# The opening of layer one: the forgetting values are projected first, 512 columns wide and one k at a time, from tokens in 256-column chunks

## The chip, the core and the metric

The kernel runs on one core of a Trainium2 chip. A time is the device time of one launch in microseconds. The core has five instruction streams that run side by side and wait for each other by semaphores: PE (TensorE: matrix products and transposes), DVE (VectorE), ACT (ScalarE), POOL (GpSimd) and SP (SyncE, which only starts transfers). In tables PEld is PE's loading of the stationary operand. Each engine takes its instructions strictly in the order in which they were written, so an instruction that waits holds up all behind it.

## The reference, cut to what matters

A decoder trunk of two layers works on 256 tokens of 1024 channels. Each layer normalises the stream, multiplies it by one wide input matrix, cuts the product into the inputs of three token mixers and their gates, and closes with branch and output projections:

```python
for layer in range(DEPTH):                       # 2
    h = rms_norm(x, norm_w[layer])               # x * rsqrt(mean(x^2) + eps) * norm_w
    proj = einsum('bsd,de->bse', h, w_in[layer]) # 1024 x 12832 columns
    (a_xbc, a_z, a_dt, b_q, b_k, b_v, b_z, c_q, c_k, c_v, c_f, c_z, gates) = split(proj)
    y_a = mamba2_branch(...)
    y_b = sliding_window_branch(b_q, b_k, b_v, b_z, ...)
    y_c = forgetting_attention_branch(c_q, c_k, c_v, c_f, c_z, ...)
    branch = einsum('bsiw,iwd->bsid', stack([y_a, y_b, y_c]), w_proj[layer])
    merged = sum(sigmoid(gates + gate_bias) * branch)
    x = x + einsum('bsd,de->bse', merged, w_out[layer])
return rms_norm(x, final_norm_w)
```

Two column groups matter here: `b_v`, the 256 sliding-window values, and `c_v`, the 1024 forgetting values (the first 512 of them above all).

## The kernel before

**Products in three parts.** Everything is float32. An operand is cut in a high part that PE's fast format holds exactly and a low part, the rest; a product of two such operands is high·high + low·high + high·low, three matrix products for each block of 128 channels. There are eight such blocks, numbered k = 0 to 7. Weights arrive in `raw` tiles of 512 KB (four k of 256 columns or two k of 512); ACT writes the high part `hi`, DVE subtracts it and writes `lo`. A `raw` buffer is free for the next transfer when its `lo` is written; there are six.

**Tokens.** The two token blocks (t = 0, 1) of 128 tokens come in as rows, in the tile `x0`. PE transposes them against the identity `ident`, DVE multiplies the transposed block by the norm weights (into `xw`), ACT writes the high part `y0.hTh`, DVE the low part `y0.hTl`. In order listings these three tiles have the pool's name L and a number, as have all tiles of a shared pool. Only later, when the sums of squares are done, is the row factor `y0.rn` known; the first projections are scaled by it when they leave PSUM, and `normalize` then multiplies `xw` by it for all that follow.

**The order of work.** The opening of the program is written out by hand for all engines in a `manual_schedule` block: small functions issue one step each. `turn` transposes, `high` and `low` write the parts of the tokens, `w_high` and `w_low` those of half a weight tile, `square` sums squares, `hh`, `lh`, `hl` issue matrix products. `parts` are the first weight tiles; `first` are the two PSUM tiles (one per token block) that the first projection fills. Those products are only evicted later, through the list `late`. After that block the projections run from the list `ops`, one after another: `u_bv` makes sliding-window values, `u_cv` forgetting values, `u_gate` gates, `u_bk` the first rotated keys. `release` returns buffers of weight parts; `load_to` and `load_part` start weight transfers on SP. The rest of the program (some 95% of the time) is ordered by the same list and by a planner that puts attention steps between projections.

**The opening before.** SP first loads token block 0 in two transfers of 512 columns, then weights, then token block 1 whole. PE spends the time until the tokens land on seven transposes of the identity (`WARM`), and ten more (`FILL`) between the tokens' transposes and the first product. The first projection is `b_v`, 256 columns: token block 0 runs through k = 0 to 3 and 4 to 7, with the transposes of block 1 in its middle, then token block 1. Then come `c_v` columns 0 to 255 and 256 to 511, 256 at a time, the gates of the sliding-window branch 512 columns at a time, two transposes of the rotation table, and the keys.

Of the kernel before, what the change touches and what calls it, by code (L numbers as in the profile page):

```python
# [11 lines left out]
F32 = mybir.dt.float32  # L12
# [22 lines left out]
WARM = 7  # L35
FILL = 10
# [14 lines left out]
def hybrid_trunk(  # L51
# [131 lines left out]
    nc.scalar.dma_start(nw8, norm_w[0:1, :].rearrange("o (k p) -> (o k) p", p=P))  # L183
    tab = T("tab", [P, 1])
    nc.vector.memset(tab, 0.0)
    act(tab, tab, AF.Exp)
    x0 = T("L8", [P, 2, D])
    for j in range(2):
        nc.sync.dma_start(x0[:, 0, j * 512:(j + 1) * 512], x2[0:P, j * 512:(j + 1) * 512])
# [10 lines left out]
    one = T("L1", [P, P])  # L200
    nc.gpsimd.memset(one, 1.0)
    onesr = T("ones", [P, P], F32R)
    nc.gpsimd.tensor_copy(onesr, one)
    ones = onesr.bitcast(F32)

# [70 lines left out]
    def ordered(ap):  # L276

        return ap.rearrange("p (i a) -> p a i", a=2)
# [245 lines left out]
    def u_bv(y, t, placed=None):  # L524

        def f(w):
            p = tok(y.hTh, y.hTl, w, t, mid=pump) if placed is None else ordered(placed[t][:, 0:w.n])
            if t == 0:
                y.bv = T("bias", [P, 2, 256])
            (late.append if placed is not None else lambda g: g())(lambda: evict(p))  # L530

        def evict(p):
# [494 lines left out]
    def u_cv(y, c, t, i=None):  # L1027

        def f(w):
            p = tok(y.hTh, y.hTl, w, t)  # L1030
            if y.cv is None:
                y.cv = T("L8", [P, 2, D])
            m = w.n if i is None else w.n - 16
# [237 lines left out]
    for y in layers:  # L1271
# [11 lines left out]
        def cols(c0, n=256):  # L1283
            return sub([(0, w[:, c0:c0 + n])], n)
# [140 lines left out]
    with tc.manual_schedule(engines={ENG.PE, ENG.DVE, ENG.Activation, ENG.Pool}):  # L1425
        load_to(2)
# [3 lines left out]
        load_to(N_RAW)  # L1430
        warm = pmx()
        for i in range(WARM):
            transpose(warm[:, 0:P], ident, ident)


        nwT = T("L1", [P, NK])
        p = pmx()
        transpose(p[:, 0:NK], nw8, ident[:NK, :NK])
        nc.vector.tensor_copy(nwT, p[:, 0:NK])
# [3 lines left out]
        ss = T("ss", [P, 4], bufs=4)  # L1443

        def turn(t, j):
            p = pmx()
            for k in range(4):
                c = j * 512 + k * P
                transpose(p[:, k * P:(k + 1) * P], x0[:, t, c:c + P], ident)
            ks = slice(4 * j, 4 * j + 4)  # L1450
            tt(xw[:, t, ks, :], p.rearrange("p (k t) -> p k t", k=4), bc(nwT[:, ks], 2, P), op=ALU.mult)

        def high(t, j):
            ks = slice(4 * j, 4 * j + 4)
            act(y0.hTh[:, t, ks, :], xw[:, t, ks, :], AF.Copy)

        def low(t, j):
            ks = slice(4 * j, 4 * j + 4)
            tt(y0.hTl[:, t, ks, :], xw[:, t, ks, :], y0.hTh[:, t, ks, :].bitcast(F32), op=ALU.subtract)
# [15 lines left out]
        parts = [new_part() for _ in range(4)]  # L1475
        first.extend((pmx(), pmm()))

        def keys(t, k0, a, b, ends=False):

            for k in range(k0, k0 + 4):  # L1480
                mm(first[t][:, 0:256], a[:, t, k, :], in_turn(b(k)),
                   start=(k == 0 and a is y0.hTh and not ends), stop=(k == NK - 1 and ends))

        w0 = pieces[0]

        def hh(t, k0):
            keys(t, k0, y0.hTh, w0.hi)

        def lh(t, k0):
            keys(t, k0, y0.hTl, w0.hi)  # L1490

        def hl(t, k0):
            keys(t, k0, y0.hTh, w0.lo, True)

        square(0, 0)
        turn(0, 0)
        high(0, 0)
        w_high(parts[0], 0)
        turn(0, 1)
        for i in range(FILL):  # L1500
            transpose(warm[:, 0:P], ident, ident)
        low(0, 0)
        w_high(parts[0], 1)
        high(0, 1)
        w_low(parts[0], 0)
        w_low(parts[0], 1)
        w_high(parts[1], 0)
        w_high(parts[1], 1)
        low(0, 1)
        w_low(parts[1], 0)  # L1510
        w_low(parts[1], 1)
        hh(0, 0)
        lh(0, 0)
        hl(0, 0)
        hh(0, 4)
        turn(1, 0)
        turn(1, 1)
        lh(0, 4)
        square(0, 1)
        high(1, 0)  # L1520
        high(1, 1)
        low(1, 0)
        low(1, 1)
        hl(0, 4)
        hh(1, 0)
        lh(1, 0)
        hl(1, 0)
        hh(1, 4)
        lh(1, 4)
        hl(1, 4)  # L1530
        for i in range(2):
            w_high(parts[2], i)
            w_low(parts[2], i)
        square(1, 0)
        square(1, 1)
# [5 lines left out]
        for part in parts[3:]:  # L1541
            for i in range(2):
                w_high(part, i)
                w_low(part, i)
# [8 lines left out]
        release(pieces[0], 2)  # L1553
# [38 lines left out]
```

## Time and profile before

| | |
|---|---|
| median of three runs | 806.76 us (806.67 to 806.95) |
| span of the profiled execution, first to last instruction | 805.1 us |
| what lies around the span (median less span) | 1.7 us |
| PE busy | 796.5 us, 99% of the span, 5160 products |
| DVE busy | 684.2 us, 85% |
| ACT busy | 533.8 us, 66% |
| POOL busy | 167.5 us, 21% |
| moved from memory | 154.71 MB, 195 GB/s over the span |

The profile gives no time of its own for the profiled execution but its span, so the 1.7 us around it are taken as the same in every run. In a timeline row the first number is the start in us from the span's start, the second the time until the group's last instruction ended, then engine, source line, operation, tiles (written<-read), shapes, and the count. Idle time ahead of a row stands in brackets with what ended it. Durations of matrix products overlap: the time one costs is the distance between two starts.

### The profile page before, as it was taken

To read this page: it belongs to the slowest core of one execution; us is meant where nothing else is said; L and a number is where in the kernel's file an instruction comes from. 1 tells how busy PE (TensorE), PEld (TensorE's weight loads), DVE (VectorE), ACT (ScalarE), POOL (GpSimd) and SP (SyncE) were. 2 spreads that over 40 slices of the span, in tenths; PEclk is the share of its full clock that TensorE was granted. 3 is DMA by queue.
4 is the path that set the end of the run, shared out by engine and by line. 5 is a ranking of instruction groups with operands and counts; after the bars stand their busy time and mean duration, and the time that the engine had idled before them with its cause. 6 is when DMAs were issued, how large, how long until landed. Compare 5 with 4: busy or idle time off the path is not lost.

```text
span 805.1 us, 14840 instructions
## 1 busy us (share of the span) xinstructions
PE 796.5 (99%) x5160; PEld 711.6 (88%) x5160; DVE 684.2 (85%) x1416; ACT 533.8 (66%) x1146; POOL 167.5 (21%) x236
## 2 busy tenths in 40 slices
PE   9999999999999999999999999999999999999996
PEld 8998988888998988888998899888889989888896
DVE  6878999997998997795785799999889999969865
ACT  7776768875775885543665678687657768755452
POOL 3166213140210100033001741122311220002000
PEclk9999999999999999999999999999999999999999
DMA  9997987797765565686678987679976546576632
GB/s 316 280 259 172 253 219 200 219 290 220 198 184 167 174 187 170 219 253 205 217 251 257 239 210 217 157 217 287 285 211 196 183 143 202 156 248 210 209 106 78
DMA packets 138827, 170.43 MB, mean 212 GB/s; under 512 B 9353, under 2 KB 106465, under 8 KB 138753
## 3 DMA queue, kind: packets, MB, share of 16 engines
q1 hardware_dynamic: 114960, 140.53, 55.5%
q0 software_dynamic: 13328, 13.29, 10.3%
q10 hardware_dynamic: 10464, 15.67, 6.7%
q8 instruction: 41, 0.67, 0.3%
q14 instruction: 34, 0.27, 0.1%
HBM read 154.71 MB, written 2.16 MB: 195 GB/s over the span
## 4 chain that ended last, share of the span: by engine, by line
PE 91%; issue 3%; DMA 2%; POOL 2%; DVE 1%; ACT 1%; POOLq 0%; DVEq 0%
PE mm L109 78%; PE mx L109 9%; PE mx L113 4%; DMA L<-L 1%; DMA hb<-in_sinks_dram 1%; POOL L L488 1%; DMA L<-in_x_dram 0%; DVE L L551 0%; ACT pp L610 0%; POOL L L285 0%; POOL L L562 0%; DVE lo L291 0%; POOL sm L224 0%; POOL L L571 0%; POOL L L572 0%
## 5 line engine op out<-in xcount | busy, mean ns | idle before, releaser
L109 PE MATMUL mm<-L,hi 128*128 128x512 f32 x1056 | 354.7, 387 | 0.5 <-ACT L L487 0.3
L291 DVE TENSOR_TENSOR lo<-raw,hi 128x1024 fp32r<-128x1024 f32 (+1 forms) x276 | 313.3, 1154 | 40.9 <-ACT hi L290 36.1
L109 PE MATMUL mm<-hi,L 128*128 128x512 f32 (+2 forms) x1168 | 303.1, 349 | 0.1
L290 ACT ACTIVATE hi<-raw 128x1024 fp32r<-128x1024 f32 (+1 forms) x276 | 265.6, 982 | 50.6 <-PE mm L109 30.0
L109 PE MATMUL mm<-L,lo 128*128 128x256 f32 x1056 | 266.6, 273 | 0.0
L109 PEld LDWEIGHTS mm<-hi,L 128*128 128x128 f32 x1168 | 205.8, 190 | 23.2 <-issue 1.5
L109 PEld LDWEIGHTS mm<-L,hi 128*128 128x128 f32 x1056 | 195.1, 190 | 27.4 <-issue 3.0
L109 PEld LDWEIGHTS mm<-L,lo 128*128 128x128 f32 x1056 | 202.1, 191 | 5.3
L109 PE MATMUL mm<-lo,L 128*128 128x512 f32 (+2 forms) x584 | 201.5, 347 | 0.0
L109 PEld LDWEIGHTS mm<-lo,L 128*128 128x128 f32 x584 | 110.2, 190 | 10.7
L488 POOL DMA_DIRECT2D L<-L x68 | 60.7, 915 | 192.5 <-ACT L L487 155.2
L1074 POOL TENSOR_SCALAR_AFFINE_SELECT bias<-bias 128x128 f32<-128x128 f32 x64 | 30.8, 513 | 82.7 <-DMA bias<-cumd 82.7
L829 DVE SCALAR_TENSOR_TENSOR L<-L,vec,L 128x255 f32<-128x255 f32 (+2 forms) x96 | 46.2, 481 | 1.9 <-ACT L L826 0.4
L486 ACT ACTIVATE L<-mm 128x256 f32<-128x256 f32 x84 | 31.9, 380 | 20.0 <-PE mm L109 14.0
L652 ACT ACTIVATE pp<-pp,nm 128x128 f32<-128x128 f32 x64 | 28.2, 443 | 22.8 <-DVE nm L646 22.8
L1109 ACT ACTIVATE L<-L 128x512 f32<-128x512 f32 x24 | 15.1, 631 | 34.5 <-DVE L L1106 30.8
L610 ACT ACTIVATE pp<-pp,nm 128x128 f32<-128x128 f32 x32 | 12.6, 394 | 24.9 <-DVE nm L615 24.1
L488 POOL DMA_DIRECT2D qt<-L x16 | 14.2, 925 | 71.4 <-ACT qt L487 64.6
L1142 POOL TENSOR_TENSOR L<-L,L 128x512 f32<-128x512 f32 x8 | 12.0, 1494 | 74.0 <-DVE L L1141 74.0
L487 ACT ACTIVATE L<-mm 128x256 f32<-128x256 f32 x68 | 26.2, 386 | 1.5 <-DMA L<-L 1.5
L1106 DVE TENSOR_TENSOR L<-mm,L 128x512 f32<-128x512 f32 x22 | 15.1, 687 | 11.2 <-PE mm L109 11.2
L551 DVE TENSOR_TENSOR L<-L,cs 128x256 f32<-128x256 f32 x40 | 20.0, 536 | 4.6 <-DMA L<-L 4.6
(213 smaller groups left out, 913.7 us busy)
## 6 DMA issues: line engine op xcount, KB each, us to landing
raw<-in_w_in_dram SPq DMA_DIRECT2D x191, 512.0 KB, 5.1
raw<-in_w_proj_dram SPq DMA_DIRECT2D x48, 512.0 KB, 6.0
L<-L POOLq DMA_DIRECT2D x72, 128.0 KB, 5.4
raw<-in_w_out_dram SPq DMA_DIRECT2D x16, 512.0 KB, 5.9
bias<-cumd ACTq DMA_DIRECT2D x16, 256.0 KB, 3.4
L<-cumd ACTq DMA_DIRECT2D x8, 512.0 KB, 5.4
L<-in_gate_bias_dram ACTq DMA_DIRECT2D x12, 256.0 KB, 5.4
qt<-L POOLq DMA_DIRECT2D x16, 128.0 KB, 6.0
```

The lines of the kernel that those rows point to most:

```text
L109: nc.tensor.matmul(o, a, b, **kw)
L113: nc.tensor.transpose(o, a, i)
L290: keep(act)(hi, src, AF.Copy)
L291: keep(tt)(lo, src, hi.bitcast(F32), op=ALU.subtract)
L486: act(halves(lo), ordered(p[:, S:2 * S]), AF.Copy)
L487: last = act(halves(out), ordered(p[:, 0:S]), AF.Copy)
L488: nc.gpsimd.dma_start(out, lo, accum_op=ALU.add)
L551: tt(m, p, cs[:, i, :], op=ALU.mult)
L652: act(pp[:, i, sl], pp[:, i, sl], AF.Exp, scale=-1.0, bias=nm[:, e:e + 1], accum_out=sums[:, e:e + 1])
L829: stt(a[:, s:S], x_[:, 0:S - s], y.vec[:, 16 * j + u:16 * j + u + 1], a[:, s:S], op0=ALU.mult, op1=ALU.add)
L1074: nc.gpsimd.affine_select(out=bias[:, i, dst], in_=bias[:, i, src], compare_op=ALU.is_ge, fill=NEG, base=0, pattern=[[-1, P]], channel_mul ...
L1106: tt(halves(g), p, halves(y.gb), op=ALU.add)
```

## The change

Six things are edited, all in the opening of layer one; the order of all later work is as before, apart from where two small products of `normalize` fall.

- **What is projected first.** The first two PSUM tiles now hold `c_v`, 512 columns at once, instead of `b_v`, 256 columns. `b_v` follows it, 256 columns wide, as an ordinary projection; `c_v`'s eviction is the late one (`u_cv` takes `placed`, `u_bv` loses it). The first weights are so 2 MB instead of 1 MB, in four parts of two k each (`FIRST`), each part loaded as two transfers of one k, the very first on ACT's queue.
- **By single k.** Products run one k at a time, for both token blocks (`both`), instead of four k for one block.
- **Tokens.** They are loaded as 256, 256 and 512 columns of both blocks, between the weight transfers, and transposed, weighted and split in chunks of 256 columns (two k): `turn`, `weigh`, `high`, `low` of chunk c.
- **Warming.** The identity transposes are gone. Instead `stir` multiplies a constant tile of ones by itself, 256 columns wide, eight, three and two times, between the first transposes.
- **Constants.** The tile of ones is made by DVE at the start instead of by POOL after other masks, and ACT's loading of its function table stands behind its first two transfers.
- **Evictions.** The first evictions are two of 512 columns; `b_v`'s are behind them.

```diff
-WARM = 7
-FILL = 10
+WARM = (8, 3, 2)
+FIRST = 4
...
+one = T("L1", [P, P])
+nc.vector.memset(one, 1.0)
+onesr = T("ones", [P, P], F32R)
+nc.vector.tensor_copy(onesr, one)
...
-        step_ = kper // 2 if j == 0 else kper
+        step_ = kper // 2 if j < FIRST else kper
...
-                nc.sync.dma_start(raw[:, h:h + step_, c:c + m],
+                (nc.scalar if j == h == 0 else nc.sync).dma_start(raw[:, h:h + step_, c:c + m],
...
-            v, cv0, cv1 = cols(C_BV), cols(C_CV), cols(C_CV + 256)
-            op(v, *(u_bv(y, t, first) for t in range(2)))
+            cv0, v = cols(C_CV, 512), cols(C_BV)
+            op(cv0, *(u_cv(y, 0, t, placed=first) for t in range(2)))
             op(None, lambda: layer_consts(y0, nc.gpsimd))
             op(None, lambda: launch(9, normalize(y0), 0.0))
-            op(cv0, u_cv(y, 0, 0), u_cv(y, 0, 1))
-            op(cv1, u_cv(y, 256, 0), u_cv(y, 256, 1))
+            op(v, *(u_bv(y, t) for t in range(2)))
...
+        tokens_in(0, 0, 256)
+        tokens_in(1, 0, 256)
+        load_to(1)
+        act(tab, tab, AF.Exp)
+        tokens_in(0, 256, 256)
+        tokens_in(1, 256, 256)
         load_to(2)
-        nc.sync.dma_start(x0[:, 1, :], x2[P:S, :])
+        tokens_in(0, 512, 512)
+        tokens_in(1, 512, 512)
+        load_to(N_RAW)
...
+        def stir(n):
+            for i in range(n):
+                mm(warm[:, 0:256], onesr, onesr.unsqueeze(1).to_broadcast([P, 2, P]), start=True, stop=True)
...
+        def hh(t, k):
+            mm(first[t], y0.hTh[:, t, k, :], in_turn(w0.hi(k)), start=(k == 0), stop=False)
...
+        stir(WARM[0])
...
+        turn(0, 0)
+        stir(WARM[1])
+        turn(1, 0)
+        stir(WARM[2])
+        weigh(0, t0)
+        high(0, t0)
+        weigh(0, t1)
+        low(0, t0)
+        w_high(parts[0], 0)
+        hh(0, 0)
...
+        for c in (2, 3):
+            turn(0, c)
+            turn(1, c)
+            weigh(c)
+            high(c)
+            if c == 2:
+                both(hh, 3)
+                both(lh, 3)
+                both(hl, 3)
+            low(c)
+            for i in range(2):
+                w_high(parts[c], i)
+                w_low(parts[c], i)
+            square(c - 2, 1)
+        for k in range(4, NK):
+            both(hh, k)
+            both(lh, k)
+            both(hl, k)
```

PE, the start of the program before: `mx_115` is the warming tile, `mx_143` and `mx_151` take the transposed tokens `L_3`, `mx_139` is the first projection's tile for token block 0, read with the high part `L_23`.

```order
L113 MATMUL mx_115<-ident_71 128x128 [waits Pool_49]
L113 MATMUL mx_115<-ident_71 128x128 x6
L113 MATMUL mx_124<-ident_71,L_1_63 128x8 [waits DMAHW0_49]
L113 MATMUL mx_143<-ident_71,L_3_68 128x128 [waits DMAHW1_49]
L113 MATMUL mx_143<-ident_71,L_3_68 128x128 x3
L113 MATMUL mx_151<-ident_71,L_3_68 128x128 [waits DMAHW2_49]
L113 MATMUL mx_151<-ident_71,L_3_68 128x128 x3
L113 MATMUL mx_115<-ident_71 128x128 x10
L109 MATMUL mx_139<-hi_131,L_23_128 128x256 [waits Activation_49]
```

PE, the same place in the changed program: `mx_121` is the warming tile, `mx_150` takes the transposed tokens `L_5`, `mx_153` and `mm_154` are the first projection's tiles for token blocks 0 and 1, read with the high part `L_22` and the low part `L_23`.

```order
L109 MATMUL mx_121<-ones_67 128x256 x7
L113 MATMUL mx_147<-ident_72,L_1_63 128x8 [waits DMAHW0_49,Pool_49]
L113 MATMUL mx_150<-ident_72,L_5_71 128x128 [waits DMAHW1_49]
L113 MATMUL mx_150<-ident_72,L_5_71 128x128
L109 MATMUL mx_121<-ones_67 128x256 x3
L113 MATMUL mx_150<-ident_72,L_5_71 128x128 [waits DMAHW3_49]
L113 MATMUL mx_150<-ident_72,L_5_71 128x128
L109 MATMUL mx_121<-ones_67 128x256 x2
L109 MATMUL mx_153<-hi_127,L_22_124 128x512 [waits Activation_49]
L109 MATMUL mx_153<-hi_127,L_23_125 128x512 [waits DVE_49]
L109 MATMUL mm_154<-hi_127,L_22_124 128x512 [waits Activation_49]
L109 MATMUL mx_153<-lo_128,L_22_124 128x512 [waits DVE_49]
```

What moved: the eight transposes of 128 columns ahead of the first product are four, the filler behind them is two products instead of ten transposes, and each of the first products waits for its own step of ACT or DVE.

DVE in the opening before: L1451 weights transposed tokens by the norm, L1459 writes the tokens' low part, L1470 a weight's low part.

```order
L1451 TENSOR_TENSOR L_22_127<-mx_143,L_20_123 128x512 [waits DVE_49,PE_49]
L1451 TENSOR_TENSOR L_22_127<-mx_151,L_20_123 128x512 [waits PE_49]
L1459 TENSOR_TENSOR L_24_129<-L_22_127,L_23_128 128x512 [waits Activation_49]
L1470 TENSOR_TENSOR lo_132<-raw_99,hi_131 128x512 [waits DMAHW3_49,Activation_49]
L1470 TENSOR_TENSOR lo_132<-raw_99,hi_131 128x512 [waits DMAHW4_49,Activation_49]
L1459 TENSOR_TENSOR L_24_129<-L_22_127,L_23_128 128x512 [waits Activation_49]
```

DVE in the changed opening, from the second chunk on: L1463 is `weigh`, L1471 `low`, L1482 `w_low`; `mx_178`, `mx_206` and `mx_226` are the transposed chunks 1, 2 and 3.

```order
L1463 TENSOR_TENSOR L_21_123<-mx_178,L_20_122 128x2x256 [waits PE_49]
L1482 TENSOR_TENSOR lo_130<-raw_104,hi_129 128x512 [waits DMAHW7_49,Activation_49]
L1471 TENSOR_TENSOR L_23_125<-L_21_123,L_22_124 128x2x256 [waits Activation_49]
L1482 TENSOR_TENSOR lo_130<-raw_104,hi_129 128x512 [waits DMAHW0_49,Activation_49]
L1463 TENSOR_TENSOR L_21_123<-mx_206,L_20_122 128x2x256 [waits PE_49]
L1471 TENSOR_TENSOR L_23_125<-L_21_123,L_22_124 128x2x256 [waits Activation_49]
L1482 TENSOR_TENSOR lo_132<-raw_109,hi_131 128x512 [waits DMAHW3_49,Activation_49]
L1482 TENSOR_TENSOR lo_132<-raw_109,hi_131 128x512 [waits DMAHW4_49,Activation_49]
L1463 TENSOR_TENSOR L_21_123<-mx_226,L_20_122 128x2x256 [waits PE_49]
L1471 TENSOR_TENSOR L_23_125<-L_21_123,L_22_124 128x2x256 [waits Activation_49]
```

What moved: before, both halves of a token block were weighted ahead of everything else; now each chunk's weighting stands behind the low parts of the chunk before it, and the last one (`mx_226`) behind three of them.

More of the change, by code (lines that the diff above doesn't have):

```diff
@@ L1512, in hybrid_trunk, with lh @@
[L1512 to L1525, printed above, removed]
+        parts = [new_part() for _ in range(FIRST + 2)]
+        w0 = pieces[0]
+        def hh(t, k):
+            mm(first[t], y0.hTh[:, t, k, :], in_turn(w0.hi(k)), start=(k == 0), stop=False)
+        def lh(t, k):
+            mm(first[t], y0.hTl[:, t, k, :], in_turn(w0.hi(k)), start=False, stop=False)
@@ new lines, in hl, with both @@
+        def hl(t, k):
+            mm(first[t], y0.hTh[:, t, k, :], in_turn(w0.lo(k)), start=False, stop=(k == NK - 1))
+        def both(f, k):
+            for t in range(2):
+                f(t, k)
+        t0, t1 = slice(0, 1), slice(1, 2)
+        stir(WARM[0])
+        p = pmx()
+        transpose(p[:, 0:NK], nw8, ident[:NK, :NK])
+        nc.vector.tensor_copy(nwT, p[:, 0:NK])
+        turn(0, 0)
+        first.extend((pmx(), pmm()))
+        stir(WARM[1])
+        turn(1, 0)
+        stir(WARM[2])
@@ L1526, in hybrid_trunk @@
+        weigh(0, t0)
+        high(0, t0)
+        weigh(0, t1)
+        low(0, t0)
+        w_high(parts[0], 0)
+        hh(0, 0)
+        w_low(parts[0], 0)
+        lh(0, 0)
+        high(0, t1)
+        low(0, t1)
+        hh(1, 0)
+        hl(0, 0)
+        w_high(parts[0], 1)
         lh(1, 0)
         hl(1, 0)
[L1528 to L1533, printed above, removed]
-        square(1, 0)
-        square(1, 1)
+        w_low(parts[0], 1)
@@ new lines, in hybrid_trunk @@
+        turn(0, 1)
+        turn(1, 1)
+        weigh(1)
+        square(0, 0)
+        both(hh, 1)
+        both(lh, 1)
+        both(hl, 1)
+        w_high(parts[1], 0)
+        high(1)
+        w_low(parts[1], 0)
+        low(1)
+        w_high(parts[1], 1)
+        w_low(parts[1], 1)
+        square(1, 0)
+        both(hh, 2)
+        both(lh, 2)
+        both(hl, 2)
+        for c in (2, 3):
[12 more added lines that the diff above has]
+            square(c - 2, 1)
@@ L1540, in hybrid_trunk @@
         r0 = root(v, 2)
-        for part in parts[3:]:
+        for part in parts[FIRST:]:
             for i in range(2):
```

87 lines of the change are left out of this document (28 added, 59 removed).

## The prediction

> **What bounds the kernel now.** I read the page first, then who waits for whom, then the opening as a timeline. The page (busy time of each engine; then the chain that ended last, by engine):
>
> ```profile
> span 805.1 us, 14840 instructions
> PE 796.5 (99%) x5160; PEld 711.6 (88%) x5160; DVE 684.2 (85%) x1416; ACT 533.8 (66%) x1146; POOL 167.5 (21%) x236
> PE 91%; issue 3%; DMA 2%; POOL 2%; DVE 1%; ACT 1%; POOLq 0%; DVEq 0%
> ```
>
> PE's own waits from 20 us to the end (who, for whom: us in total, times, longest):
>
> ```profile
> PE mm L109 <- ACT L L487: 0.3, 1, 0.3
> ```
>
> So PE streams from about 12 us to its end with one wait of 0.3 us. The edit stops before 40 us, and behind it the same instructions follow. Whatever the opening gains or loses arrives at the end one for one, and the question is when PE reaches a fixed later point. I take the first key product. PE's timeline up to it (start, length, count; idle time in brackets):
>
> ```profile
> 1.53 1.76 PE L113 MATMUL mx<-ident 128*128 128x128 f32 x7 [1.53 <-POOL ident masks.py:199]
> 5.35 2.25 PE L113 MATMUL mx<-ident 128*128 128x128 f32 x10
> 7.34 1.15 PE L109 MATMUL mx<-hi,L 128*128 128x256 f32 x8
> 9.54 1.04 PE L113 MATMUL mx<-ident,L 128*128 128x128 f32 x8
> 14.65 0.39 PE L109 MATMUL mm<-hi,L 128*128 128x256 f32 x2
> 22.69 0.40 PE L109 MATMUL mx<-L,ones 128*128 128x256 f32 x2
> 22.93 0.38 PE L109 MATMUL mm<-hi,L 128*128 128x256 f32 x2
> 25.61 0.60 PE L109 MATMUL mm<-hi,L 128*128 128x512 f32 x2
> 35.97 0.38 PE L113 MATMUL mx<-ident,L 128*128 128x128 f32 x2
> 36.11 0.46 PE L109 MATMUL mm<-L,hi 128*128 128x512 f32 x1
> ```
>
> The first product starts at 7.34, the first key product at 36.11: 28.77 us. Prices: from 14.65 to 25.61 lie 96 products of 256 columns and the pair of 0.24, so 10.72 / 96 = 0.112 each. From 25.61 to 35.97 lie 48 of 512 columns, 0.216 each. A transpose costs (1.04 - 0.27) / 7 = 0.11 at 9.54 us, with 0.27 the length of one, but (2.25 - 0.33) / 9 = 0.21 at 5.35: PE's clock is half until about 7.3 us. Work in the stretch: 144 x 0.1117 = 16.08; the pair 0.24; eight transposes 0.87; 48 gate products 10.36; two transposes 0.14. That is 27.69. The other 1.08 is waiting, all before 12.5 us.
>
> [...]
>
> **The steps that the opening is made of.** The other engines' rows:
>
> ```profile
> 0.81 0.59 ACTq L183 DMA_DIRECT2D L<-in_norm_w_dram  x1
> 1.44 1.28 ACT L186 ACT_TABLE_LOAD   x1 [1.44 <-PEq L1581]
> 3.22 0.18 PEld L113 LDWEIGHTS mx<-ident,L 8*128 8x128 f32 x1 [0.33 <-DMA L<-in_norm_w_dram]
> 3.53 0.17 DVE L1439 COPY L<-mx 128x8 f32<-128x8 f32 x1 [2.60 <-PE mx L113]
> 3.57 0.63 ACT L241 ACTIVATE L<-L 128x512 f32<-128x512 f32 x1 [0.63 <-DMA L<-in_x_dram]
> 4.74 0.69 DVE L1451 TENSOR_TENSOR L<-mx,L 128x512 f32<-128x512 f32 x1 [1.04 <-PE mx L113]
> 5.47 0.63 ACT L1455 ACTIVATE L<-L 128x512 fp32r<-128x512 f32 x1 [1.18 <-DVE L L1451]
> 6.00 1.14 ACT L1464 ACTIVATE hi<-raw 128x512 fp32r<-128x512 f32 x2
> 6.80 1.29 DVE L1470 TENSOR_TENSOR lo<-raw,hi 128x512 fp32r<-128x512 f32 x2
> 41.36 0.39 ACT L486 ACTIVATE L<-mm 128x256 f32<-128x256 f32 x1
> 47.49 0.76 DVE L551 TENSOR_TENSOR L<-L,cs 128x256 f32<-128x256 f32 x2
> ```
>
> A step of 512 columns takes 0.62 on ACT and the next can start after 0.52 (1.14 - 0.62); on DVE 0.69 and 0.60. At 256 columns: 0.39 on ACT; on DVE 0.42, the next after 0.34. A hand-off costs 0.04 (4.74 + 0.69 = 5.43, ACT starts at 5.47). A product that had to wait also shows its weight load; I put 0.1 for that, an estimate between nothing and the 0.19 that a load takes:
>
> ```profile
> L109 PEld LDWEIGHTS mm<-hi,L 128*128 128x128 f32 x1168 | 205.8, 190 | 23.2 <-issue 1.5
> ```
>
> **Part by part.**
>
> *The work itself.* 48 x 0.216 = 10.37 and 48 x 0.1117 = 5.36 replace 16.08: -0.35. Twelve transposes now lie behind the first product instead of eight: +0.44. The fixed work is 10.37 + 5.36 + 12 x 0.109 + 0.24 + 10.36 + 0.14 = 27.78.
>
> *The start of products.* DVE makes the ones by about 1.5 (it idles until 3.53). Eight cold stirs: no row shows one; a 256-column product takes 0.112 at full clock, and transposes doubled, so 0.21 (bounds 0.11 and 0.22): 3.2. The norm weights land then, as before; their transpose 0.2, two transposes 0.43, three stirs 0.64, two transposes 0.43: 4.9; their result 0.2 later. DVE's `weigh` serves both token blocks only then, since both sets of transposes report together. 5.1 + 0.42 + 0.04 + 0.31 (ACT's slot for `high`) + 0.62 + 0.14 = 6.6, against 7.34: -0.74. If the clock is already full, 6.1.
>
> *The first k.* Its six products are 1.30 of work. The fifth needs the second block's low part, which stands behind `w_low`: 0.04 + 0.60 + 0.42 + 0.04 after `w_high`, so 0.2 is lost; and until 7.4 products run at half speed: 0.5 in all.
>
> *Four waits that the finer steps leave* (one product 0.216, six for each k):
> - k = 2: from the last transpose, result 0.16, `weigh` 0.69, `high` 0.62, hand-offs 0.08 = 1.55, behind six products (1.30): 0.25 + 0.1.
> - Its low products: `low` ends 0.77 after `high`; two products and the reload cover 0.53: 0.24, rounded with the next reload to 0.3.
> - k = 4: 0.16 + 0.69 + 0.52 + 0.62 + 0.08 = 2.07, behind six products and four transposes (1.74): 0.33 + 0.1.
> - k = 6: the last `weigh` stands behind three low parts on DVE. From the end of chunk 2's `high`: 3 x 0.60 + 0.69, then 0.52 + 0.62, hand-offs 0.12 = 3.75; PE started k = 4 at 0.66 and has twelve products (2.59): 0.5 + 0.1.
> Together 1.75.
>
> *At nothing.* ACT's second transfer moves its table load back by 0.5; it ends at about 3.3, and ACT's first step is due at 5.6. Without that cover, 0.5. The row factor and the constants come some 5 us later; POOL's first rotation transfer waits 14.6 us for ACT (below), so 9 are left. `normalize` falls among the gates; its eight steps of 0.69 on DVE end about 1.5 us before the keys, and each 0.1 beyond that would cost 0.1. `c_v`'s bank must be evicted before the gates, two ACT steps behind the row factor: 1.5 to spare.
>
> ```profile
> POOL L L488 <- ACT L L487: 19.2, 5, 14.6
> ```
>
> *Weights.* 3.1 MB of tokens and weights must land for the first projection. Transfer rates by stretch (last figure, GB/s):
>
> ```profile
> 0.00:5.00 5.00, 3.37 (x15) 2.94 (x16) 0.48 (x3) 2.21 (x4) 2.35 (x15) 1.00 0.58 176
> 5.00:10.00 5.00, 4.97 (x34) 4.78 (x33) 4.81 (x8) 3.96 (x8) 0.00 (x0) 1.00 1.04 356
> 10.00:15.00 5.00, 4.87 (x42) 4.48 (x41) 4.16 (x9) 4.09 (x10) 0.05 (x1) 1.00 1.10 348
> raw<-in_w_in_dram SPq DMA_DIRECT2D x2, 256.0 KB, 4.2
> raw<-in_w_in_dram SPq DMA_DIRECT2D x11, 512.0 KB, 7.4
> ```
>
> 0.88 + 1.78 MB by 10 us, the rest by 11.4, needed at 17. The third weight piece (1.3 MB in) is there at about 7, needed at 8: hidden, with 1 us to spare.
>
> **The sum.** 6.6 + 27.78 + 0.5 + 1.75 = 36.6, against 36.11: +0.5. The profiled execution's span goes from 805.1 to 805.6, and with the 1.7 around it the median from 806.76 to 807.3. In steps: start -0.74, work -0.35, transposes +0.44, first k +0.5, waits 1.75 for 1.08, +0.67. A difference of 0.2%, 1.6 us, is about what a measurement of this kernel can tell from no change; the forecast is below it.
>
> **Rivals.**
>
> *The clock stays half until 10.3 or later (slower).* Before, PE worked from 3.59 without a break until the clock doubled, 3.7 us. Now there is a hole, from 5.3 (last stir) to 6.6. If unbroken work is what counts, the clock doubles at 10.3 to 10.8. Three more us or so at half speed lose 1.5 to 1.7 of work; the waits of k = 2 swallow some 0.4: +1.2 on top, 36.11 + 1.7, 808.5; between 808.1 and 808.9. It decides from the point where the doubling falls after about 8. For it: the hole. Against: before, 5.3 us of transposes preceded the doubling, gaps and all; by that sum it would come at about 8.1. Chance 0.34, three quarters of it above 808.4.
> [...]
>
> *The clock doubles early, at about 4 to 5.* Products may count for more than transposes. Then the start is 6.1 and the first k loses 0.2: 36.6 - 0.5 - 0.3 = 35.8, 806.5. Chance 0.16.
>
> *The waits do not arise (faster).* If the steps overlap better than priced and the clock is early too, 35.8 - 1.75 = 34.1: 804.8. Against it: DVE's and ACT's rows are measured. Chance 0.07.
>
> *Weights land late (slower).* If the single-k pieces take the 7.4 us of the large ones, the third, issued at about 2.9, lands at 10.3 instead of being used at 8.1: +2.2, 809.5. Against it: before, two pieces of that size took 4.2. Chance 0.08.
>
> **How the numbers follow.** The forecast has 0.35 and is the likeliest: 807.3. Within 0.2% lie forecast, early clock and a quarter of the late one: 0.35 + 0.16 + 0.09 = 0.60. Slower: 0.25 + 0.08 = 0.33. Faster 0.07. The range leaves out waits that vanish and late weights: 806.1 (early clock, with the three stirs at 0.11 and no reloads behind the waits: 0.4 less) to 808.9 (late clock).
>
> **What would show it.** First 512-column product at 6.6; its neighbours 0.21 (full) or 0.43 (half) apart tell the clock; PE idle ahead of k = 2, 4 and 6 on ACT, and before the low products of k = 2 on DVE; gates' first product at about 26.1 and the first key product at 36.6. A first key product before 35.5, or PE waiting for a transfer, would make the account wrong.

## The result and the profile after

The changed kernel takes 810.02 us (median of five, 808.12 to 811.14), the kernel before 806.80 (806.67 to 807.29): a ratio of 1.0034 on record, 95% interval 1.0023 to 1.0046 (the two medians alone give 1.0040). It is slower, and by more than the range of the forecast allowed (806.1 to 808.9). The profiled execution took 810.88, one of the longer ones. Its page (span, TensorE's line, the chain that ended last):

```profile
span 809.2 us, 14756 instructions
PE 797.8 (99%) x5108; PEld 709.7 (88%) x5108; DVE 685.1 (85%) x1422; ACT 533.3 (66%) x1147; POOL 168.0 (21%) x234
PE 92%; DVE 4%; ACT 2%; issue 1%; DMA 1%; ACTq 0%; DVEq 0%
```

TensorE is still the bound. TensorE's timeline, first the opening, then its end (the last row is its last product), and the same last row of before:

```profile
1.42 2.07 PE L109 MATMUL mx<-ones 128*128 128x256 f32 x8 [1.42 <-DVE ones L187]
3.96 0.99 PE L109 MATMUL mx<-ones 128*128 128x256 f32 x3
4.95 0.69 PE L113 MATMUL mx<-ident,L 128*128 128x128 f32 x2
5.28 0.77 PE L109 MATMUL mx<-ones 128*128 128x256 f32 x2
7.11 1.22 PE L109 MATMUL mx<-hi,L 128*128 128x512 f32 x2 [1.06 <-ACT hi L1476]
8.13 0.63 PE L109 MATMUL mm<-hi,L 128*128 128x512 f32 x1
8.56 0.63 PE L109 MATMUL mx<-lo,L 128*128 128x512 f32 x1
10.93 0.38 PE L109 MATMUL mm<-hi,L 128*128 128x512 f32 x1
...
38.57 0.46 PE L109 MATMUL mm<-L,hi 128*128 128x512 f32 x1
...
802.43 0.28 PE L109 MATMUL mm<-lo,L 128*128 128x256 f32 x1
```

```profile
798.56 0.28 PE L109 MATMUL mm<-lo,L 128*128 128x256 f32 x1
```

The first product starts at 7.11 (forecast 6.6), and products last 0.63 and stand 0.43 apart: half clock. From 10.93 they last 0.38. The trace's clock record has full speed from 10.73, against 7.39 before; ahead of that it has no entry, so the half clock is read from the spacing. The first key product starts at 38.57, not at 36.6. And the end has moved further than that: from the first key product to TensorE's end it takes 802.71 - 38.57 = 764.14, before 798.84 - 36.11 = 762.73.

So the span's 4.0 us divide into three: the start of products, 7.11 for 7.34, -0.23 (forecast -0.74); from there to the first key product, 31.46 for 28.77, +2.69 (forecast +1.23); and the rest, +1.41 with 0.15 more behind TensorE's end (forecast nothing). TensorE's waits behind 38 us (who, for whom: us in total, times, longest) show where the third lies; before there was one wait of 0.3:

```profile
PE mm L109 <- ACT L L483: 0.9, 2, 0.6
PE mm L109 <- DVE L L1104: 0.7, 2, 0.4
```

The first of them in the timeline, before and then after. ACTq rows are ScalarE issuing transfers:

```profile
125.00 1.07 ACT L290 ACTIVATE hi<-raw 128x1024 fp32r<-128x1024 f32 x1
125.15 0.81 ACTq L810 DMA_DIRECT2D cumd<-L  x2
126.01 0.39 ACT L486 ACTIVATE L<-mm 128x256 f32<-128x256 f32 x1
```

```profile
126.88 1.07 ACT L286 ACTIVATE hi<-raw 128x1024 fp32r<-128x1024 f32 x1
127.03 1.95 ACTq L803 DMA_DIRECT2D cumd<-L  x2
129.03 0.38 ACT L482 ACTIVATE L<-mm 128x256 f32<-128x256 f32 x1 [1.07 <-PE mm L109]
129.31 0.38 ACT L483 ACTIVATE L<-mm 128x256 f32<-128x256 f32 x1
129.74 0.48 PE L109 MATMUL mm<-L,hi 128*128 128x512 f32 x1 [0.55 <-ACT L L483]
```

ScalarE issues the two transfers of the running gate sums (`cumd`) in 1.95 us instead of 0.81; the second alone takes 1.58 for 0.45. The eviction behind them starts when the issue is done, and the next product has no free PSUM bank until it is evicted (it waits 0.55). The row blames a product for ScalarE's 1.07 of idle time, but that is only the product that happened to end last, at 128.97: in e6 below, where ScalarE's issue is short, the same eviction starts eight products sooner. What it waits for here is the issue, which ends at 128.98. Layer two has the same place at 523 us, with 1.40. What runs there shows in the DMA queues' packets of the same two microseconds, before (125.2 to 127.2) and after (126.9 to 128.9); columns: packets, MB, share of 16 engines:

```profile
q0 software_dynamic: 144, 0.13, 47.0%
q10 hardware_dynamic: 96, 0.03, 6.7%
```

```profile
q0 software_dynamic: 139, 0.13, 46.0%
q8 instruction: 1, 0.02, 4.1%
q10 hardware_dynamic: 45, 0.02, 3.5%
q14 instruction: 1, 0.01, 1.7%
```

Two transfers of the kind instruction, 16 KB on q8 at 127.3 and 8 KB on q14 at 127.6, lie on the issue; before, the nearest lie 6.6 us ahead of it and 7.4 behind.

### The profile page after: what moved, and what is told of

Its sections match the earlier page's. It is cut to its first block, busy times and chain, and to the rows that moved or that the text cites. A ratio compares the mean times of both kernels' runs of the same rounds, so it can differ in the third digit from the quotient of the medians.

```text
span 809.2 us, 14756 instructions
## 1 busy us (share of the span) xinstructions
PE 797.8 (99%) x5108; PEld 709.7 (88%) x5108; DVE 685.1 (85%) x1422; ACT 533.3 (66%) x1147; POOL 168.0 (21%) x234
## 3 DMA queue, kind: packets, MB, share of 16 engines
q0 software_dynamic: 13328, 13.29, 10.3%
## 4 chain that ended last, share of the span: by engine, by line
PE 92%; DVE 4%; ACT 2%; issue 1%; DMA 1%; ACTq 0%; DVEq 0%
PE mm L109 79%; PE mx L109 9%; PE mx L113 3%; DVE lo L287 1%; DVE L L822 1%; DMA raw<-in_w_in_dram 1%; ACT pp L603 0%; ACT hi L286 0%; DVE pp L608 0%; ACTq L803 0%; DVE L L1104 0%; DVE pp L632 0%; DVE L L774 0%; ACT hi L1476 0%; DVE L L1463 0%
## 5 line engine op out<-in xcount | busy, mean ns | idle before, releaser
L287 DVE TENSOR_TENSOR lo<-raw,hi 128x1024 fp32r<-128x1024 f32 (+2 forms) x274 | 310.8, 1153 | 37.8 <-ACT hi L286 34.6
L286 ACT ACTIVATE hi<-raw 128x1024 fp32r<-128x1024 f32 (+2 forms) x274 | 263.8, 983 | 50.7 <-PE mm L109 34.4
L109 PEld LDWEIGHTS mm<-hi,L 128*128 128x128 f32 x1136 | 202.4, 190 | 23.1 <-issue 1.7
L109 PE MATMUL mm<-lo,L 128*128 128x512 f32 (+2 forms) x568 | 199.1, 351 | 0.0
L109 PEld LDWEIGHTS mm<-lo,L 128*128 128x128 f32 x568 | 107.8, 190 | 10.9
L109 PE MATMUL mx<-hi,L 128*128 128x512 f32 x80 | 26.2, 396 | 1.8 <-ACT hi L1476 1.6
```

The source lines that it names most:

```text
L109: nc.tensor.matmul(o, a, b, **kw)
L286: keep(act)(hi, src, AF.Copy)
L287: keep(tt)(lo, src, hi.bitcast(F32), op=ALU.subtract)
```

## The experiments

Two theories come out of this. *Clock*: the hole of TensorE ahead of the first product put the doubling off. *Fetch*: transfers of the kind instruction come in step with the engines' streams (before, 41 of 16 KB on q8 for 10472 recorded instructions of TensorE, 255 each), and since the change alters how many instructions stand ahead, a fetch now falls on an issue that TensorE waits for. Against both stand simpler causes: the extra transfer on ScalarE's queue, a clock that ignores the hole, a mere shift in time.

All runs, each number from its profile but for the times. Issues are the second `cumd` issues of the two layers; "behind" is from the first key product to TensorE's end; "small" are transposes of 8 columns (see e9).

| kernel | median (range) us | first product | full clock from | first key product | behind | issues |
|---|---|---|---|---|---|---|
| before | 806.80 (806.67-807.29) | 7.34 | 7.39 | 36.11 | 762.7 | 0.45, 0.45 |
| after | 810.02 (808.12-811.14) | 7.11 | 10.73 | 38.57 | 764.1 | 1.58, 1.40 |
| e1 after, SP queue | 810.17 (809.00-811.13) | 6.86 | 6.05 | 36.75 | 764.1 | 1.53, 1.12 |
| e2 after, more stirs | 810.48 (808.54-811.03) | 7.51 | 7.37 | 37.39 | 765.5 | 1.59, 0.95 |
| e3 before, hole | 807.98 (807.25-808.22) | 6.97 | 12.31 | 38.03 | 762.2 | 0.45, 0.45 |
| e4 before, ACT queue | 807.26 (806.73-807.37) | 7.45 | 7.17 | 36.40 | 762.4 | 0.44, 0.45 |
| e5 after, memsets | 810.37 (809.53-812.48) | 7.16 | 5.16 | 37.05 | 765.1 | 1.55, 1.09 |
| e6 after, issue on SP | 808.88 (807.88-810.52) | 6.87 | 5.36 | 36.75 | 763.7 | on SP: 0.35, 0.34 |
| e7 before, memsets | 807.44 (806.93-808.04) | 7.70 | 9.27 | 37.20 | 762.1 | 0.45, 0.45 |
| e8 after, stirs, memsets | 809.61 (807.88-810.82) | 7.52 | 6.74 | 37.40 | 763.5 | 1.55, 0.44 |
| e9 after, 52 small | 813.40 (810.72-813.70) | 11.38 | 16.87 | 43.05 | 762.2 | 0.72, 0.66 |
| e10 before, 77 small | 817.26 (816.01-818.23) | 15.90 | 19.95 | 46.26 | 763.8 | 1.58, 1.10 |
| e11 before, 128 small | 820.82 (819.21-821.31) | 18.90 | 22.50 | 49.05 | 762.1 | 0.45, 0.45 |
| e12 after, narrow stirs | 813.41 (812.58-813.92) | 11.07 | 15.03 | 42.48 | 762.9 | 0.44, 0.45 |
| e13 after, both cures | 807.97 (807.61-808.22) | 7.13 | 5.33 | 37.48 | 762.2 | 0.45, 0.45 |

**e1, the weight piece back on SyncE's queue**

```diff
-  (nc.scalar if j == h == 0 else nc.sync).dma_start(raw[...
+  nc.sync.dma_start(raw[...
```

> The changed kernel with the first half of the first weight piece back on SyncE's queue; nothing else differs. Of the 4.1 us that the changed kernel's span has gained, 2.5 are there at the first key product, and the rest comes from waits behind 40 us (1.6 us in four waits against 0.3 before), in the two places where ScalarE issues the second transfer of the running gate sums: 1.40 and 1.58 us for that issue, against 0.45 before. Theory A (the extra transfer on ScalarE's queue makes that issue long): it is back at 0.45 here, the waits behind 40 us fall to about 0.3, median 808.7, 1.3 less than the changed kernel. Rival B (the issue is long because of when it falls against other traffic, and the queue of the weight piece has nothing to do with it): still 1.4 to 1.6, median 810.0 within 0.5. Either way the first product moves by no more than 0.3.

Measured: issues of 1.53 and 1.12, median 810.17. The queue is not it. The profile brought something else: here the clock doubled at 6.05 although TensorE's opening is that of the changed kernel, hole and all. In e6, which does not touch the opening at all, it doubled at 5.36. The same opening thus reaches the first key product at 36.75 (e1 and e6) or at 38.57, by the run. TensorE's rows here:

```profile
6.86 0.70 PE L109 MATMUL mx<-hi,L 128*128 128x512 f32 x2 [1.06 <-ACT hi L1476]
...
13.94 0.60 PE L113 MATMUL mx<-ident,L 128*128 128x128 f32 x4
14.77 0.48 PE L109 MATMUL mx<-hi,L 128*128 128x512 f32 x1 [0.23 <-ACT hi L1476]
15.09 0.38 PE L109 MATMUL mm<-hi,L 128*128 128x512 f32 x1
...
36.75 0.46 PE L109 MATMUL mm<-L,hi 128*128 128x512 f32 x1
```

**e2, the hole filled**

```diff
-WARM = (8, 3, 2)
+WARM = (9, 5, 8)
```

> The changed kernel with 9, 5 and 8 stirs for 8, 3 and 2, so that TensorE works from 1.4 us to the first product with no hole over 0.2 us; at the spacing of 0.213 the last ends at about 7.2. Theory A (the doubling of the clock needs some 3.7 us of unbroken work; the hole from 5.7 to 7.1 us put it off to 10.7): products are 0.216 apart from the first or within half a microsecond of it, the first key product is at 37.1 to 37.4 instead of 38.57, median 808.7, 1.3 less than the changed kernel. Rival B (the doubling comes at points that this work does not move): it stays at 10 to 11 us, first key product at 38.6, median 810.0.

Clock full at 7.37, ahead of the first product; first key product at 37.39, as theory A had it. The median did not follow: the stretch behind it grew to 765.5. Issues of 1.59 and 0.95 again, and a new wait of 0.89 at 408 us. Some 17 us ahead of that, ScalarE issued a load of `x` for 1.72 us, on top of another 16 KB fetch (391.3 us); that the wait follows from it was not tried.

**e3, a hole in the old opening**

```diff
-FILL = 10
+FILL = 0
```

> The kernel before without its ten filling transposes, so that TensorE has a hole of some 2 us ahead of the first product at 7.34. Theory A (unbroken work): the clock doubles 3.3 us later or more, at 10.7 or above; products at half speed between 7.3 and then lose (10.7 - 7.3) / 2 = 1.7, of which its waits there swallow some; first key product at 37.2 to 37.8, median 808.1, 1.3 more than the kernel before. Rival B (the clock does not hang on the filling): first key product at 36.1, median 806.8.

Clock full only at 12.31, first key product at 38.03, later than the 37.8 that I had allowed; ratio 1.0011 (1.0002 to 1.0020). With a hole of 1.11 us ahead of the first product the clock came 4.9 us later in the old kernel too. The profile loses 1.9 up to the first key product and is 0.6 faster behind it (762.2 for 762.7); the median loses 1.0.

**e4, the weight piece on ScalarE's queue, in the old kernel**

```diff
-  nc.sync.dma_start(raw[...
+  (nc.scalar if j == h == 0 else nc.sync).dma_start(raw[...
```

> The kernel before with one line changed: the first half of its first weight piece is issued on ScalarE's queue instead of SyncE's. Theory A (that extra transfer makes the later issue of the second gate sums long): 1.4 to 1.6 us instead of 0.45 in both layers, new waits of TensorE behind 40 us of about 1.3 in all, median 808.0. Rival B (it has nothing to do with the queue): 0.45, median 806.8 within 0.3.

0.44 and 0.45, 807.26: theory A falls here as in e1.

**e5, VectorE's fetch moved**

```diff
+    pad = T("pad", [P, 1])
+    for _ in range(10):
+        nc.vector.memset(pad, 0.0)
```

> The changed kernel with ten one-column memsets (0.06 us each) more on VectorE in its opening, where VectorE idles from 1.4 to 3.7 us. They do no work; they shift VectorE's later instructions by ten places in its instruction stream. The first trace showed two transfers of the kind instruction, 16 KB and 8 KB, at 127.3 and 127.6 us and again at 523.3 and 523.4, each time on top of ScalarE's long issue of the second transfer of gate sums (1.58 and 1.40 us); in the kernel before none falls there, and the issue takes 0.45. The 8 KB ones come whenever VectorE has run 128 more instructions. Theory A (a fetch of VectorE's instructions that falls on the issue makes it long): here that fetch comes some 3 us earlier, the issue takes 0.45, or about 1.0 if the 16 KB fetch for TensorE, which stays, counts as well; TensorE's waits behind 40 us fall from 1.66 to below 0.8, and the median by 0.6 to 1.4, to 809.0. Rival B (the fetches only happen to be there): still 1.4 to 1.6, median 810.1.

The 8 KB fetch came at 124.4 instead of 127.6: it is VectorE's. (In the trace of before, twelve transfers of 8 KB on q14 from 132.9 to 736.3 us stand 121 to 133 of VectorE's recorded instructions apart, its issues and waits counted.) The issues stayed at 1.55 and 1.09 with the 16 KB fetch alone on them, above the 1.0 that I had named. VectorE's fetch is not the main part. The stretch behind grew to 765.1, with new waits of TensorE at 76, 101 and 126 us (0.26, 0.57 and 0.27), whose cause stays open.

**e6, the issue moved to SyncE**

```diff
-  nc.scalar.dma_start(y.cumd[:, :, c * P:(c + 1) * P]...
+  (nc.scalar, nc.sync)[c].dma_start(y.cumd[:, :, c * P:(c + 1) * P]...
```

> The changed kernel with the second of the two gate-sum transfers of each layer issued by SyncE instead of ScalarE; the fetches stay where they are. Theory A (what costs is that ScalarE stands at this issue for 1.4 to 1.6 us, and evictions behind it keep a PSUM bank from TensorE): ScalarE is free 1.4 us earlier, TensorE's waits at 129.7 and 525.4 (0.55 and 0.36) vanish, those at 153.7 and 549.6 (0.28 and 0.40) too if they follow from it; median 809.0 to 809.4, 0.7 to 1.2 less. Rival B (the waits come from elsewhere): same waits, median 810.1.

Median 808.88, 1.1 less than the changed kernel, but the intervals of the two ratios overlap (1.0016 to 1.0033 here, 1.0023 to 1.0046 there). The fetch still comes, at 125.78, 0.16 us into the two issues, and both keep their length. The waits at 129.7 and 525.4 are gone: those two do come from ScalarE standing at its issue. The two later ones, on VectorE, stay or grow (0.76 at 152.0, 0.41 at 547.3), and the stretch behind is 763.7, only 0.4 less. So this is half a confirmation, and by what way the fetch leads to the later waits stays open.

**e7, a fetch put on the issue in the old kernel, missed**

```diff
+    for _ in range(17):
+        nc.vector.memset(pad, 0.0)
```

> The kernel before with 17 one-column memsets more on VectorE in its opening, where it idles from 0.9 to 3.5 us; they shift VectorE's stream so that its fetch, which came when 326 of its recorded instructions had begun, comes at the instruction that runs at the second gate-sum issue (308 begun). Theory A (the fetch on top of the issue is what makes it long): the issue takes 0.9 to 1.0 here instead of 0.45 in both layers, new waits of 0.3 to 0.8 in all, median 807.3 to 807.7. Rival B: 0.45, median 807.0 within 0.2.

The 17 memsets moved VectorE's fetch too far: it came at 122.9, 3.1 us ahead of the issue at 126.0, where it had come 7.4 behind it. Nothing collided, so nothing was tested. The issue stayed at 0.45.

**e8, stirs and memsets**: the edits of e2 and e5 together.

> [...] In the run with the stirs alone the clock doubled at 7.37 and the first key product came at 37.39, 1.2 earlier than in the changed kernel's profile. Theory A (two causes, each with its own cure): first key product at 37.4, gate-sum issues at 0.45 to 1.0, median 808.2 within 0.5, and a spread of its runs of under 1 us against 3. Rival B (the later waits come anyway, in other places): median above 809.3.

Rival B by the median, but the trace splits the two layers. In layer one the 16 KB fetch lay on the issue: 1.55. In layer two it came 6.0 us earlier (516.5 for 522.5) and no fetch was near: 0.44. Queues' packets from 126.1 and from 522.1 us on, two microseconds each:

```profile
q0 software_dynamic: 140, 0.13, 47.2%
q8 instruction: 1, 0.02, 4.4%
q10 hardware_dynamic: 45, 0.02, 3.5%
```

```profile
q0 software_dynamic: 144, 0.13, 47.2%
q10 hardware_dynamic: 96, 0.03, 7.0%
```

**e9, e10 and e11, TensorE's stream shifted.** Small transposes, whose results nothing reads, move every later instruction of TensorE; n is 52 in the changed kernel, ahead of its first product, and 77 and 128 in the old one, ahead of its filling transposes.

```diff
+        for i in range(n):
+            transpose(warm[:, 0:8], ident[0:8, :], ident[:8, :8])
```

> The changed kernel with 52 transposes of 8 columns more on TensorE, ahead of the first product, whose results nothing reads. The changed kernel has 52 matmuls fewer than the kernel before, so from here on every later instruction of TensorE stands at the same place of its stream as before, and the 16 KB fetches of its instructions fall on the same places of the program as before (the one ahead of the gate sums 6.5 us before their second issue instead of on it). The ten memsets of the run before had moved the 8 KB fetch away and left the 16 KB one, and the issue stayed long (1.55 and 1.09); in the run with memsets and stirs the 16 KB fetch of layer two was elsewhere, and there the issue took 0.44. Theory A (TensorE's fetch on top of the issue, and the 8 KB one less so): issues of 0.45 in layer one and 0.45 to 1.0 in layer two, where the 8 KB fetch remains; from the first key product to TensorE's end 762.2 to 763.2 us, against 764.1 in the changed kernel and 762.1 to 762.7 in four kernels built on the one before. Rival B (something else in the changed opening): 764 or more. The opening itself may be longer by the 52 transposes, up to 3 us, so the median says little.

> The kernel before with 77 such transposes more ahead of its filling ones: 154 instructions, which brings TensorE's later stream to the alignment of the changed kernel (154 + 103 = 257, a fetch of 256 and one). Theory A: the 16 KB fetch falls on the second issue of the gate sums in both layers, which then takes 0.9 to 1.4 us instead of 0.45, and from the first key product to TensorE's end it takes 763.2 to 764.2 us. Rival B: 0.45, and 762.1 to 762.7 us. The opening is longer by the 77 transposes in any case.

> The same kernel with 128 such transposes: 256 instructions, a whole fetch, so that the alignment is that of the kernel before, with a still longer opening. Theory A: issues of 0.45 in both layers, 762.1 to 762.7 us from the first key product to TensorE's end. If a later start of everything is what made the issue long, it is long here too, and the stretch 763 or more.

The stretches behind the first key product came out as theory A had them in all three. The issues did in e11; e9's of layer one is longer than the 0.45 expected, and e10's of layer one longer than 1.4. ScalarE's issues of layer one in the timelines of e9, e10 and e11, in turn:

```profile
131.49 1.08 ACTq L803 DMA_DIRECT2D cumd<-L  x2
```

```profile
134.73 1.95 ACTq L810 DMA_DIRECT2D cumd<-L  x2
```

```profile
137.48 0.81 ACTq L810 DMA_DIRECT2D cumd<-L  x2
```

And the queues' packets in two microseconds from 131.4 us (e9), 134.6 (e10) and 137.4 (e11):

```profile
q10 hardware_dynamic: 96, 0.03, 7.3%
q14 instruction: 1, 0.01, 1.3%
```

```profile
q8 instruction: 1, 0.02, 4.3%
q10 hardware_dynamic: 45, 0.02, 3.5%
```

```profile
q10 hardware_dynamic: 96, 0.03, 6.8%
```

The changed kernel with the old alignment has lost its 16 KB fetch there; with only VectorE's left, the issues take 0.72 and 0.66, and it needs 762.2 behind the first key product. The old kernel with the changed kernel's alignment has the fetch, issues of 1.58 and 1.10, waits of TensorE of 1.2 and 763.8. With 256 instructions more, and a still later start, it is the old kernel again: 0.45, 0.45, 762.1. This shows in both directions that the place of TensorE's fetch is the cause of what is lost behind the first key product; a mere shift in time is ruled out by e11. e11 fits the count of before, 255 recorded instructions of TensorE for each 16 KB.

**e12, both cures at a little price**: e5's memsets, and the stirs at half the width and in larger number.

```diff
-WARM = (8, 3, 2)
+WARM = (18, 8, 14)
-  mm(warm[:, 0:256], onesr, onesr.unsqueeze(1).to_broadcast([P, 2, P]), ...)
+  mm(warm[:, 0:P], onesr, onesr, ...)
```

> The changed kernel with both cures at little price: its stirs are 128 columns wide and 18, 8 and 14 in number (for 8, 3 and 2 of 256), so that the hole ahead of the first product is filled and TensorE's later stream moves by 54 instructions, and VectorE has ten memsets more in its opening. No row shows a stir of 128 columns; if it takes half of the 0.213, the stirs last as long as 9, 4 and 7 wide ones, and the first product comes at 7.1 to 7.5. Theory A (a hole in a clock window and a fetch on the gate-sum issue were the two costs): clock doubled by 8.3 at the latest in every run, first key product 29.9 after the first product, at 37.0 to 37.4; issues of 0.45; 762.2 to 762.7 from there to TensorE's end; median 807.6 within 0.4, spread of its runs under 1.2 us. That is 0.5 to 1.2 above the kernel before. Rival B (the two causes are not all): median 808.5 or more. If 128 columns take as long as 256, the first product comes at 9 to 10, and only the stretch behind the first key product tells.

A stir of 128 columns takes as long as one of 256 (18 in 4.11 us, against 9 in 2.29 in e2), so the first product came at 11.07 and the median tells nothing. Full clock came at 15.03, not by 8.3; that time, like the clock window of theory A, was an estimate of mine that no run shows. Issues of 0.44 and 0.45, 762.9 behind.

**e13, both cures in idle time**: WARM = (9, 4, 8), e5's memsets, and 19 small transposes inside TensorE's waits ahead of k = 2, 4 and 6.

```diff
+        small(1, 3)
         both(hh, 2)
...
         for k in range(4, NK):
+            small(*{4: (2, 6), 6: (3, 10)}.get(k, (0, 0)))
             both(hh, k)
```

> The changed kernel with stirs of 256 columns, 9, 4 and 8 of them, ten memsets more on VectorE, and 19 transposes of 8 columns more on TensorE that stand in its waits ahead of k = 2, 4 and 6 (3, 6 and 10 of them): 54 instructions more in all, as many as in the run with narrow stirs, where the issues took 0.44 and 0.45. At full clock a transpose of 8 columns is put at 0.054, half of the 0.109 that 52 of them took at half clock (5.65 us); the waits there are 0.15, 0.23 and 0.34, so some 0.3 of them shows. Theory A (hole and fetch were the two costs, and nothing third): first product at 7.2 to 7.5, clock doubled by 8.3 in every run, first key product at 37.2 to 37.7, issues of 0.45, 762.1 to 762.9 from there to TensorE's end, median 807.9 within 0.4, spread of its runs under 1.2 us against 3. Rival B (a third cause): median 808.6 or more, or a spread of 2 us and more.

Median 807.97 in eleven runs, 807.61 to 808.22; ratio to the kernel before 1.0011 (1.0002 to 1.0020). TensorE's rows, its only wait behind 37 us, and ScalarE's issues:

```profile
5.40 1.19 PE L109 MATMUL mx<-ones 128*128 128x256 f32 x8
7.13 0.70 PE L109 MATMUL mx<-hi,L 128*128 128x512 f32 x2 [0.54 <-ACT hi L1479]
14.73 0.53 PE L113 MATMUL mx<-ident 8*128 8x8 f32 x6
17.98 0.78 PE L113 MATMUL mx<-ident 8*128 8x8 f32 x10
```

```profile
PE mm L109 <- DVE L L1107: 0.2, 1, 0.2
```

```profile
125.91 0.81 ACTq L806 DMA_DIRECT2D cumd<-L  x2
```

Both costs are gone, the spread falls from 3.0 us to 0.6, and what is left is 1.0 over the kernel before: there is no third cause of size. No run here beats the kernel before, and none points to one that would.

**When the clock doubles.** In the trace's clock record full clock is an entry of 795.305 us in the kernel before and in the changed kernel alike; where it begins differs from run to run. TensorE's rows for six profiles, with the start of the work without a gap that leads up to it (in e1 that work ends at 5.81):

| profile | works without a gap from | full clock from | us between |
|---|---|---|---|
| e13 | 1.42 | 5.33 | 3.91 |
| e1 | 1.42 | 6.05 | 4.63 |
| e2 | 1.42 | 7.37 | 5.95 |
| before | 3.59 | 7.39 | 3.80 |
| after | 7.11 | 10.73 | 3.62 |
| e3 | 6.97 | 12.31 | 5.34 |

The length of unbroken work alone does not tell when: in the changed kernel TensorE worked from 1.42 to 6.05 without a gap, 4.6 us, and the clock stayed half, while in e13 it doubled 3.9 us after the first stir. The changed kernel, e1, e5 and e6 have the same stirs, with a hole of 1.06 us behind them in the changed kernel and in e1, and full clock came at 10.73, 6.05, 5.16 and 5.36. What decides between these no run shows. e9 to e12, where TensorE ran transposes of 8 columns or narrow stirs, are in the last section.

## Why the prediction was wrong, step by step

**Everything behind the first key product arrives one for one: this step failed.** It took 1.41 us more there, with the same instructions in the same order, and TensorE's waits there grew from 0.31 to 1.59: 0.91 behind ScalarE's two long issues, 0.68 by a way that stays open. What differs is where in TensorE's stream the 16 KB fetches fall, since 52 products fewer stand ahead (5108 for 5160). I had argued from the order alone; the profile of before has the instruction queues in its DMA part, and I did not ask what falls on them. e10 and e11 show it in the old kernel: 763.8 and 762.1.

**The clock: the forecast took the wrong branch.** The forecast had full clock from 7.4; the rival with 10.3 to 10.8 had 0.34 and a price of 1.2. It came at 10.73 and cost 31.46 - 29.88 = 1.58, with 29.88 the stretch from first product to first key product in every profile of this opening with full clock from the start (e1, e2, e5, e6, e8). The argument against it, that the sum of earlier work counts, "gaps and all", was wrong: in the changed kernel 4.6 us of work ahead of the hole and 3.6 behind it went by before full clock, against the 5.3 that I had counted before. That the same opening can have full clock at 5.2 to 6.1 (e1, e5, e6) or at 10.73, by the run, I gave no time of its own. How often the late doubling comes among the five timed runs no trace shows.

**The start of products: right mechanism, wrong size.** 6.6 was forecast, 7.11 measured, 6.86 to 7.16 in e1, e5 and e6. The second pair of transposes was put at 4.5 and began at 4.95: it waited for the second block's tokens, which landed at 4.90; my sum had not asked when they land.

**The work, the first k and the four waits: right.** Forecast 27.78 + 0.5 + 1.75 = 30.0, measured 29.88 at full clock. In e1, from the spacings, the four waits are 0.32, 0.19, 0.40 and 0.50 and the reload behind each 0.10 (14.77 to 15.09 is 0.32, where neighbours stand 0.216 apart): 1.81, against 1.75. (The four forecast terms add up to 1.68; the 1.75 was a slip of 0.07.) For k = 4: the transposes end at 13.94 + 4 x 0.109 = 14.38, the product starts at 14.77. The first k lost 0.3.

**What was put at nothing cost nothing up to the keys.** TensorE has no wait between 19.8 us and the first key product. The table load, the late constants and `normalize` stayed hidden, and no product waited for a weight transfer: that rival fell.

**The sum, repaired.** Forecast 807.3; the start adds 0.3 to 0.5 and the clock up to 1.6 (none in e13); the fetches add 1.4 in the profile. With both taken away e13 has 807.97, of which its small transposes make 30.35 - 29.88 = 0.47.

## What to carry to other kernels

A change at the beginning of a tuned program shifts every later instruction in its engine's stream, so an instruction fetch can land on a transfer's issue far behind it (here at 127.3 us, for an edit that stops before 40): compare the instruction transfers with the issues on the path before calling the rest unchanged, and compare stretches, not totals. Fill the engine from its first instruction until real work starts, and look at the clock that this gives (products of 256 columns gave full clock at 7.37, 6.74 and 5.33 in e2, e8 and e13, products of 128 at 15.03 in e12), since with one and the same hole of 1.06 us it came at 6.05 in e1 and at 10.73, for 1.58 us, in the changed kernel. A spread of 3 us where the kernel before has 0.6 is itself a finding: something near the path differs from run to run.

## What the runs showed of the hardware that I had not expected

- With a 16 KB instruction fetch of TensorE on it, ScalarE's issue of the second gate-sum transfer took 1.09 to 1.59 us instead of 0.45; with VectorE's 8 KB fetch alone, 0.66 to 0.95 (0.72 and 0.66 in e9). In the fifteen profiles ScalarE has 18 issues of over 0.6 us past the start, and a fetch lies on each of them; 69 more of its issues overlap a fetch and stay below 0.6. What makes the difference stays open. A long issue need not cost anything: in e12 one of 1.40 at 395.5 us left TensorE without a wait.
- TensorE's busy time alone does not tell when the clock doubles. In e9, 52 transposes of 8 columns filled the profile from 5.74 to 11.38, and the clock came only at 16.87; in e11 it had come at 5.43 and was taken back at 8.85, among such transposes, until 22.50. In e12, stirs of 128 columns, as long as those of 256, kept TensorE without a gap from 1.42 to the first product at 11.07, and the clock came only at 15.03. In the kernel before it came at 7.39, and what TensorE had run until 7.34 was transposes, all but one of 128 columns.
- Prices at the small end: a transpose of 8 columns takes 0.108 at half clock (52 in 5.64 us) and some 0.06 at full ((0.78 - 0.53) / 4); half the columns of a stir save nothing (e12).
